# 32 columns of the second expert sweep move from dense to gathered, and the fifth row buffer moves into a tile of the middle stage

## The chip, the cores and the metric

The kernel runs on one core of one Trainium2 chip. Its engines are TensorE (PE; the loading of its weights is shown apart, as PEld), VectorE (DVE), ScalarE (ACT), GpSimd (POOL), and SyncE (SP), which here only issues transfers; 16 DMA engines move data between HBM and SBUF. The metric is the time of one execution on the device in microseconds (us), as a median of runs.

## The reference, cut to what matters

One encoder layer over 256 tokens of 2048 columns: an attention block, and then a mixture of 16384 one-neuron experts, of which every token uses 128 (8 heads, 16 each). The change lies in the last step, the sum of the experts' value rows:

```
u = jnp.take(expert_u, eb, axis=0)
vv = jnp.take(expert_v, eb, axis=0)
act = jax.nn.gelu(jnp.einsum('td,thkd->thk', xb, u))
return jnp.einsum('thk,thkd->td', act * gb, vv)
```

`expert_v` has 16384 rows of 2048 float32 columns. The layer ends with a residual add and an RMS norm.

## The kernel before

The stages are: input projection and attention; output projection; query projection and the search for each token's 128 experts; the first sweep, over `expert_u`; the middle stage, which turns the sums of the first sweep into one gated weight for each token and expert; and the second sweep, over `expert_v`.

**The second sweep has two halves.** The first `V1` = 1472 columns of `expert_v` are done densely: the kernel keeps a weight matrix over all 16384 experts in the arena `A` (zero where a token does not use an expert), and TensorE multiplies every expert's row by it. The other `VT` = 576 columns are done sparsely: for each of the 2 token tiles and each of a token's 128 picks, an indirect DMA gathers 128 rows (one for each token of the tile) and VectorE adds them, weighted, to a running sum.

**Dense half.** The 1472 columns are three chunks, of widths `VW` = (512, 512, 448). There are 192 units of loading (`units` = 128 blocks of experts x 3 chunks / 2). Three successive units hold two expert blocks: a unit of 1024 columns, one of 2 x 448 = 896 (`i % 3 == 1`), and another of 1024. `load_split` brings a unit into one of five `raw` buffers (SP issues it), ACT rounds it to `hi`, DVE makes `lo = raw - hi`; there are three buffers of each. Then `v_matmuls` issues 12 matmuls for a unit: two token tiles, two halves of the unit, and three products (lines 939 to 941: weight high part by `hi`, the same by `lo`, weight low part by `hi`). Over the sweep the 448-wide chunk takes 128 blocks x 2 tiles x 3 products = 768 matmuls. The six sums stay in PSUM until the end.

**Sparse half.** `fetch` takes a row buffer from the pool tile `rows` (`ROWS` = 5 buffers of 128 x 576) and issues the gather on POOL (line 649). `weigh` (line 1020) is one DVE instruction: it multiplies a landed row buffer by a column of `wN` and adds it to `vsum`. Right behind it `weigh` calls `fetch` again, so that five gathers are in flight at most, and each waits for the weighing that frees its buffer. The first five are fetched at unit `FETCH` = 4, each behind a one-column memset (`held`).

**Order.** DVE's order is written out by hand in this stage (`tc.manual_schedule(engines={DVE})`): after each unit's `lo`, `spread` puts in as many `weigh` steps as an even spread of the 256 over the remaining units gives, one or two each. DVE runs them in that order, so a `weigh` that waits for its row holds up the `lo` behind it. The other engines' orders come from the scheduler.

**The tile of the middle stage.** `h2t` is a tile of 128 x 2 x 512 float32. The first sweep reads it; then the middle stage uses its space for four arrays of 256 columns: `partT` (columns 0 to 255), `actT` (256 to 511), `wT` (512 to 767) and `wN` (768 to 1023). The first three hold sums and weights of the middle stage and are not read in the second sweep. `wN` is read by every `weigh`. `weights_of(1)` reads columns 640 to 767 just before the second sweep's gathers begin.

**The end.** At unit `units - 5` the gathered sum goes to the output tile; the last three units' matmuls are ordered by token tile; then follow, for each tile and chunk, the residual add (line 1071), squares, gain, scaling (lines 238 and 240) and the store.

Of the kernel before, what the change touches and what calls it, by code (L numbers as in the profile page):

```python
# [9 lines left out]
F32 = mybir.dt.float32  # L10
# [8 lines left out]
P = 128  # L19
# [14 lines left out]
D1 = 1536  # L34
DT = D - D1
KA = D1 // P
V1 = 1472
VT = D - V1
VW = (512, 512, V1 - 1024)
RAW = 3  # L40
# [25 lines left out]
FETCH, WEIGH, ROWS = 4, 7, 5  # L66
# [37 lines left out]
def encoder_layer_kernel(ctx: ExitStack, tc: tile.TileContext, x, gT, w_in, gq, gk, w_out, g2,  # L104
# [27 lines left out]
    def take(n, at=None):  # L132
        if at is None:
            at = pos[0]
            pos[0] += n
        assert at + n <= NK * S, at + n
        return arena[:, at:at + n]
# [77 lines left out]
    def load_gain(g):  # L215
        nc.sync.dma_start(gb, bass.AP(tensor=g.tensor, offset=g.offset, ap=[[0, P], [1, D]]))

    def v_chunk(c):
        return slice(c * 512, c * 512 + VW[c]) if c < 3 else slice(V1, D)

    squares = Ring([arena[:, 20480 + VT * i:20480 + VT * (i + 1)] for i in range(2)])

    def square_sum(t, c, ss, at=chunk):
        src = xs[:, t, at(c)]
        nc.scalar.activation(squares.next()[:, :src.shape[-1]], src, AF.Square, accum_out=ss[:, c:c + 1])
# [65 lines left out]
    rows = Ring([take(512) for _ in range(3)])  # L291
# [210 lines left out]
    h2t = consts.tile([P, NT, DT], F32, name="h2t")  # L502
# [141 lines left out]
    def held(rows_):  # L644

        nc.vector.memset(rows_[:, 0:1], 0.0)

    def gather(rows_, table, t, j):
        nc.gpsimd.indirect_dma_start(out=rows_, out_offset=None, in_=table,  # L649
                                     in_offset=bass.IndirectOffsetOnAxis(ap=experts[:, j // 32, t * 32 + j % 32:t * 32 + j % 32 + 1], axis=0))  # L650
        return rows_
# [110 lines left out]
    rows, hots, hot, one_hots = {}, {}, {}, {}  # L762
# [19 lines left out]
    with query:  # L782
        for i in range(units):
# [20 lines left out]
            while ended and (ended[0][0] <= i or i == units - 1):  # L804
                _, dst, sums = ended.popleft()
# [12 lines left out]
            while opening and opening[0][0] <= i:  # L818
                p = opening.popleft()[1]
# [185 lines left out]
    vp = ctx.enter_context(tc.tile_pool(name="vp", bufs=2))  # L1005
    raws.append((vp, MORE))
    vsum = vp.tile([P, NT, VT], F32, name="vsum", bufs=1)
    picks, coming = deque((t, j) for t in range(NT) for j in range(P)), deque()

    def fetch(hold=False):  # L1010
        if picks:
            t, j = picks.popleft()
            rows_ = vp.tile([P, VT], F32, name="rows", bufs=ROWS)
            if hold:
                held(rows_)
            coming.append((t, j, gather(rows_, v_tail, t, j)))

    def weigh():
        t, j, rows_ = coming.popleft()
        nc.vector.scalar_tensor_tensor(vsum[:, t], rows_, wN[:, t, j:j + 1], vsum[:, t], op0=OP.mult, op1=OP.add)  # L1020
        fetch()
# [6 lines left out]
    with tc.manual_schedule(engines={DVE}):  # L1028
        for i in range(units):
# [15 lines left out]
            if i == 3 * units // 4:  # L1045
                nc.sync.dma_start(xs[:, :, :V1], x2d.rearrange("p (t d) -> p t d", t=NT)[:, :, :V1])
                load_gain(gf)
                ready_sqrt()
            if i == FETCH:
                for _ in range(ROWS):  # L1050
                    fetch(hold=True)
                nc.sync.dma_start(vsum, x2d.rearrange("p (t d) -> p t d", t=NT)[:, :, V1:])
            if WEIGH <= i < units - 1:
                spread(units - 7 - i)
            if i == units - 5:
                for t in range(NT):
                    nc.vector.tensor_copy(xs[:, t, V1:], vsum[:, t])
                    square_sum(t, 3, ssl[t], v_chunk)
# [98 lines left out]
```

## Time and profile before

| | |
|---|---|
| median of 3 runs | 1644.61 us (1644.09 to 1644.99) |
| the profiled execution | 1645.29 us |
| its span, first to last instruction | 1643.5 us |
| PE busy in the span | 1621.1 us |
| DVE busy in the span | 1357.2 us |
| POOL busy in the span | 702.7 us |
| matmuls of the second sweep | from 1123.4 to 1632.9 us |
| gathers of `expert_v` | from 1137.3 to 1602.3 us |

The span is read as follows. A profile's times are those of one execution, counted from its first instruction. An engine's busy time is the time in which it works on at least one instruction; successive matmuls overlap in the records, so the pace of TensorE is read from the starts of successive matmuls rather than from the duration of one. The share of the DMA engines is the mean share of the time in which the 16 have a packet under way.

### The profile page before, as it was taken

How to read it: one execution, taken by the hardware profiler on the slowest of the kernel's cores; microseconds unless marked ns; L12 is line 12 of the kernel's file. 1: busy time of each engine (PE TensorE's matmuls, PEld its weight loads, DVE VectorE, ACT ScalarE, POOL GpSimd, SP SyncE). 2: the span in 40 equal slices, each digit the busy share in tenths (PEclk: the TensorE clock that was granted, in tenths of full speed). 3: DMA queues.
4: the chain of work that ended last, by engine and by line, in shares of the span. 5: the costliest groups of instructions: out<-in, count | busy, mean ns of one | idle time of the engine just before them, and what ended most of it. 6: DMA issues, size and time to landing. Idle time of an engine off the chain costs nothing.

```text
span 1643.5 us, 25515 instructions
## 1 busy us (share of the span) xinstructions
PE 1621.1 (99%) x8706; PEld 1403.7 (85%) x8706; DVE 1357.2 (83%) x3043; ACT 866.7 (53%) x1255; POOL 702.7 (43%) x582
## 2 busy tenths in 40 slices
PE   8999999999999999999999999999999999999997
PEld 6888888887888888888888889998888888888886
DVE  6765555559799989888888859997999999999996
ACT  6465555454444454444444448996444444444444
POOL 0000000000233368776765623334677766666670
PEclk9999999999999999999999999999999999999999
DMA  7644554565776689999999873336999999999994
GB/s 250 194 142 165 166 205 154 192 219 174 240 252 244 238 295 376 372 343 346 338 341 317 296 249 116 120 127 206 375 384 361 365 345 361 355 356 346 356 349 153
DMA packets 126163, 443.04 MB, mean 270 GB/s; under 512 B 17745, under 2 KB 18641, under 8 KB 125649
## 3 DMA queue, kind: packets, MB, share of 16 engines
q1 hardware_dynamic: 85072, 298.78, 52.0%
q0 software_dynamic: 40960, 142.64, 24.4%
q8 instruction: 68, 1.11, 0.3%
q14 instruction: 63, 0.51, 0.1%
HBM read 437.02 MB, written 4.33 MB: 269 GB/s over the span
## 4 chain that ended last, share of the span: by engine, by line
PE 92%; DVE 4%; DMA 2%; ACT 1%; issue 1%; SPq 0%; ACTq 0%; DVEq 0%
PE act L797 21%; PE act L799 11%; PE o L940 10%; PE o L941 10%; PE o L939 10%; PE pr L275 6%; PE pr L277 6%; PE pr L276 6%; PE X L854 3%; PE W L904 3%; DVE lo L171 1%; PE o1p L860 1%; PE sc L357 1%; PE po L388 1%; DMA raw<-in_w_in_dram 1%
## 5 line engine op out<-in xcount | busy, mean ns | idle before, releaser
L170 ACT ACTIVATE hi<-raw 128x1024 fp32r<-128x1024 f32 (+1 forms) x445 | 464.8, 1045 | 528.7 <-PE o L941 252.4
L171 DVE TENSOR_TENSOR lo<-raw,hi 128x1024 fp32r<-128x1024 f32 (+1 forms) x445 | 535.5, 1204 | 176.0 <-ACT hi L170 173.7
L797 PE MATMUL act<-hTa,hi 128*128 128x512 f32 x1536 | 396.9, 393 | 0.0
L649 POOL DMA_INDIRECT rows<-in_v_tail_dram,experts x256 | 323.9, 1265 | 152.5 <-DVE vsum L1020 75.8
L649 POOL DMA_INDIRECT A<-in_u_tail_dram,experts x121 | 146.9, 1214 | 467.5 <-DVE den L637 409.0
L797 PEld LDWEIGHTS act<-hTa,hi 128*128 128x128 f32 x1536 | 271.5, 189 | 44.6
L940 PE MATMUL o<-lo,wt 128*128 128x512 f32 (+1 forms) x768 | 293.2, 382 | 0.8 <-DVE lo L171 0.7
L939 PE MATMUL o<-hi,wt 128*128 128x512 f32 (+1 forms) x768 | 293.2, 382 | 0.0
L941 PE MATMUL o<-hi,wt 128*128 128x512 f32 (+1 forms) x768 | 293.0, 382 | 0.0
L649 POOL DMA_INDIRECT wm<-in_u_tail_dram,experts x135 | 174.6, 1293 | 168.2 <-DVE wm L655 122.6
L799 PEld LDWEIGHTS act<-hTa,lo 128*128 128x128 f32 x1536 | 218.2, 190 | 21.0 <-DVE lo L171 0.2
L799 PE MATMUL act<-hTa,lo 128*128 128x256 f32 x1536 | 224.4, 282 | 0.0
L1020 DVE SCALAR_TENSOR_TENSOR vsum<-rows,h2t,vsum 128x576 f32<-128x576 f32 x256 | 208.8, 816 | 13.8 <-DMA rows<-in_v_tail_dram,experts 11.0
L940 PEld LDWEIGHTS o<-lo,wt 128*128 128x128 f32 x768 | 144.2, 188 | 25.6 <-DVE lo L171 1.3
L941 PEld LDWEIGHTS o<-hi,wt 128*128 128x128 f32 x768 | 144.2, 188 | 24.4 <-DVE wt L934 0.5
L939 PEld LDWEIGHTS o<-hi,wt 128*128 128x128 f32 x768 | 144.2, 188 | 24.1
L275 PE MATMUL pr<-hi,hTa 128*128 128x512 f32 x408 | 164.2, 404 | 0.0
L276 PE MATMUL pr<-lo,hTa 128*128 128x512 f32 x408 | 160.1, 392 | 0.3
L277 PE MATMUL pr<-hi,hTa 128*128 128x512 f32 x408 | 159.5, 391 | 0.0
L170 ACT ACTIVATE hi<-A 128x1024 fp32r<-128x1024 f32 x72 | 76.6, 1065 | 72.6 <-PE act L797 52.0
L171 DVE TENSOR_TENSOR lo<-A,hi 128x1024 fp32r<-128x1024 f32 x72 | 88.1, 1223 | 20.7 <-ACT hi L170 20.5
L897 POOL TENSOR_SCALAR o<-cs,I2T,h2t 128x128 f32<-128x128 f32 x64 | 54.7, 860 | 115.0 <-DVE h2t L888 56.6
(161 smaller groups left out, 2002.9 us busy)
## 6 DMA issues: line engine op xcount, KB each, us to landing
raw<-in_v_head_dram SPq DMA_DIRECT2D x128, 512.0 KB, 5.5
raw<-in_u_head_dram SPq DMA_DIRECT2D x120, 512.0 KB, 5.3
raw<-in_w_in_dram SPq DMA_DIRECT2D x72, 512.0 KB, 3.3
A<-in_u_head_dram SPq DMA_DIRECT2D x72, 512.0 KB, 5.3
raw<-in_v_head_dram SPq DMA_DIRECT2D x64, 448.0 KB, 5.8
raw<-in_w_out_dram SPq DMA_DIRECT2D x32, 512.0 KB, 3.3
raw<-in_w_query_dram SPq DMA_DIRECT2D x32, 512.0 KB, 3.7
bc<-i1d SPq DMA_DIRECT2D x32, 512.0 KB, 3.7
```

The source lines that it names most:

```text
L170: nc.scalar.activation(hi, raw, AF.Copy)
L171: nc.vector.tensor_tensor(lo, raw, hi.bitcast(F32), op=OP.subtract)
L275: nc.tensor.matmul(ps[t], xT(k, 0, r), hi[:, c], start=first, stop=False)
L276: nc.tensor.matmul(ps[t], xT(k, 0, r), lo[:, c], start=False, stop=False)
L277: nc.tensor.matmul(ps[t], xT(k, 1, r), hi[:, c], start=False, stop=last)
L649: nc.gpsimd.indirect_dma_start(out=rows_, out_offset=None, in_=table, in_offset=bass.IndirectOffsetOnAxis(ap=experts[:, j // 32, t * 32 + ...
L797: nc.tensor.matmul(ps, hi[:, c], h, start=k == 0, stop=False)
L799: nc.tensor.matmul(ps[:, :S], lo[:, c], hTs(k, 0, slice(0, S)), start=False, stop=k == KA - 1)
L939: nc.tensor.matmul(ps, w[:, 0, r], hi[:, c], start=e == 0, stop=False)
L940: nc.tensor.matmul(ps, w[:, 0, r], lo[:, c], start=False, stop=False)
L941: nc.tensor.matmul(ps, w[:, 1, r], hi[:, c], start=False, stop=e == NK - 1)
L1020: nc.vector.scalar_tensor_tensor(vsum[:, t], rows_, wN[:, t, j:j + 1], vsum[:, t], op0=OP.mult, op1=OP.add)
```

## The change

Three numbers follow from `V1`: the dense part has 1440 columns, its third chunk is 416 wide, and `VT`, the gathered part, is 608 wide. The unit `i % 3 == 1` is loaded as 832 columns, the rows of the gathered table are 2432 bytes long in place of 2304, and the boundary between the two parts of the output moves with them. The number of units, matmuls, gathers and weighings stays as it is. Four row buffers stay in the pool `vp`; the fifth is the first 608 columns of `h2t`, so it covers `partT`, `actT` and the first 96 columns of `wT`. A ring hands out the five in turn.

```
-V1 = 1472
+V1 = 1440
...
     vsum = vp.tile([P, NT, VT], F32, name="vsum", bufs=1)
+
+    row_bufs = Ring([vp.tile([P, VT], F32, name="rows", bufs=ROWS - 1) for _ in range(ROWS - 1)]
+                    + [h2t.rearrange("p t d -> p (t d)")[:, :VT]])
...
-            rows_ = vp.tile([P, VT], F32, name="rows", bufs=ROWS)
+            rows_ = row_bufs.next()
```

## Rows read from the trace of the kernel before

**Rows 1.** The page, its first part: busy time of each engine, share of the span, instructions.

```profile
PE 1621.1 (99%) x8706; PEld 1403.7 (85%) x8706; DVE 1357.2 (83%) x3043; ACT 866.7 (53%) x1255; POOL 702.7 (43%) x582
```

**Rows 2.** The page, its fourth part: the chain of work that ended last, share of the span by engine.

```profile
PE 92%; DVE 4%; DMA 2%; ACT 1%; issue 1%; SPq 0%; ACTq 0%; DVEq 0%
```

**Rows 3.** Four stretches of the second sweep: busy time of each engine and its instructions, then the granted TensorE clock, the share of the DMA engines and what they moved.

```profile
1160.00:1250.00 90.00, 90.00 (x412) 77.09 (x412) 81.83 (x95) 42.17 (x47) 63.33 (x50) 1.00 1.01 381
1250.00:1350.00 100.00, 100.00 (x458) 85.70 (x457) 92.07 (x107) 45.91 (x51) 70.72 (x56) 1.00 0.98 356
1350.00:1450.00 100.00, 100.00 (x458) 85.81 (x457) 92.92 (x107) 46.58 (x52) 69.48 (x56) 1.00 0.98 356
1450.00:1550.00 100.00, 100.00 (x458) 85.62 (x457) 91.94 (x106) 47.55 (x54) 67.21 (x56) 1.00 0.97 351
```

**Rows 4.** Groups of instructions by line and shape, 1120 to 1640 us: count, busy us, mean ns of one, idle time of the engine before them and what ended it.

```profile
L649 POOL DMA_INDIRECT rows<-in_v_tail_dram,experts x256 | 323.9, 1265 | 152.5 <-DVE vsum L1020 75.8 <-issue 43.4 <-DMA rows<-in_v_tail_dram,experts 11.7
L1020 DVE SCALAR_TENSOR_TENSOR vsum<-rows,h2t,vsum 128x576 f32<-128x576 f32 x256 | 208.8, 816 | 13.8 <-DMA rows<-in_v_tail_dram,experts 11.0
L940 PE MATMUL o<-lo,wt 128*128 128x512 f32 x512 | 199.7, 390 | 0.8 <-DVE lo L171 0.7
L171 DVE TENSOR_TENSOR lo<-raw,hi 128x1024 fp32r<-128x1024 f32 x126 | 154.0, 1223 | 34.2 <-ACT hi L170 33.3
...
L940 PE MATMUL o<-lo,wt 128*128 128x448 f32 x256 | 93.5, 365 | 0.0
...
L171 DVE TENSOR_TENSOR lo<-raw,hi 128x896 fp32r<-128x896 f32 x63 | 68.3, 1084 | 1.0 <-ACT hi L170 1.0
...
L238 ACT ACTIVATE A<-A,rstd 128x576 f32<-128x576 f32 x2 | 1.5, 768 | 0.0
...
L1071 DVE TENSOR_TENSOR A<-A,o 128x448 f32<-128x448 f32 x2 | 1.2, 614 | 0.0
```

**Rows 5.** Timeline of all engines from 1400 us (start us, us, what): the first of 24 matmuls of 512 columns, the first of the 12 of 448 columns behind them, and the next of 512.

```profile
1401.57 0.39 PE L939 MATMUL o<-hi,wt 128*128 128x512 f32 x1
...
1407.02 0.36 PE L939 MATMUL o<-hi,wt 128*128 128x448 f32 x1
...
1409.45 0.39 PE L939 MATMUL o<-hi,wt 128*128 128x512 f32 x1
```

**Rows 6.** Timeline of TensorE in the first sweep, from 900 us: eight matmuls of 256 columns in one row, and the row behind it.

```profile
901.76 1.11 PE L799 MATMUL act<-hTa,lo 128*128 128x256 f32 x8
902.71 1.09 PE L797 MATMUL act<-hTa,hi 128*128 128x512 f32 x4
```

**Rows 7.** Groups of weight loads over the whole span: the loads of those 256-column matmuls.

```profile
L799 PEld LDWEIGHTS act<-hTa,lo 128*128 128x128 f32 x1536 | 218.2, 190 | 21.0 <-DVE lo L171 0.2
```

**Rows 8.** What DVE waited for, 1160 to 1250 us: us in total, times, longest.

```profile
DVE vsum L1020 <- DMA rows<-in_v_tail_dram,experts: 5.6, 6, 1.9
```

**Rows 9.** The same, 1300 to 1500 us.

```profile
DVE vsum L1020 <- DMA rows<-in_v_tail_dram,experts: 1.5, 3, 0.5
```

**Rows 10.** Timeline of DVE around 1224 us: a weighing that waited for its row, and the `lo` of a 448-wide unit behind it.

```profile
1223.53 0.82 DVE L1020 SCALAR_TENSOR_TENSOR vsum<-rows,h2t,vsum 128x576 f32<-128x576 f32 x1 [1.94 <-DMA rows<-in_v_tail_dram,experts]
1224.26 1.08 DVE L171 TENSOR_TENSOR lo<-raw,hi 128x896 fp32r<-128x896 f32 x1
```

**Rows 11.** Timeline of TensorE there: the first matmul that reads that `lo`.

```profile
1225.83 0.37 PE L940 MATMUL o<-lo,wt 128*128 128x448 f32 x1
```

**Rows 12.** Transfers, 1160 to 1250 us: the sum, and the gathers with the median time from issue to landing.

```profile
DMA packets 9267, 34.31 MB, mean 381 GB/s; under 512 B 1364, under 2 KB 1364, under 8 KB 9132
...
rows<-in_v_tail_dram,experts POOLq DMA_INDIRECT x50, 6.8
```

**Rows 13.** The same, 1300 to 1500 us.

```profile
DMA packets 19780, 70.89 MB, mean 354 GB/s; under 512 B 2981, under 2 KB 2981, under 8 KB 19766
...
rows<-in_v_tail_dram,experts POOLq DMA_INDIRECT x111, 6.0
```

**Rows 14.** Transfers, 1150 to 1600 us: the sum, and each queue's packets, MB and share of the 16 engines' time (q1: the dense units; q0: the gathers).

```profile
DMA packets 44842, 161.72 MB, mean 359 GB/s; under 512 B 6714, under 2 KB 6714, under 8 KB 44681
...
q1 hardware_dynamic: 25152, 88.85, 52.3%
q0 software_dynamic: 19657, 72.47, 45.9%
```

**Rows 15.** All waits of 1120 to 1643 us: the longest of a matmul of the second sweep for its `lo`.

```profile
PE o L940 <- DVE lo L171: 0.7, 1, 0.7
```

**Rows 16.** What writes and reads the arena `A`, 700 to 980 us: duration min/median/max, first and last start; and, after the list of what these instructions waited for, the gathers' time to landing.

```profile
L649 POOL DMA_INDIRECT A<-in_u_tail_dram,experts x76: 945/1152/1937, 700.4 to 918.6; - x76
...
L803 ACT ACTIVATE A<-act x66: 380/400/411, 702.9 to 976.7; 128x256 f32<-128x256 f32 x66
...
  PE act L799: 42.2, 33
...
DMA to landing us min/median/max: 3.9/5.8/7.8
```

**Rows 17.** The two transposes of `wT` by `weights_of` (whole span).

```profile
L909 PE MATMUL wtp<-cs,h2t x2: 272/274/275, 1059.8 to 1130.8; 128*128 128x128 f32 x2
```

**Rows 18.** What writes and reads the row buffers (whole span).

```profile
L649 POOL DMA_INDIRECT rows<-in_v_tail_dram,experts x256: 942/1402/1942, 1137.3 to 1602.3; - x128
L1020 DVE SCALAR_TENSOR_TENSOR vsum<-rows,h2t,vsum x256: 805/812/882, 1144.0 to 1609.8; 128x576 f32<-128x576 f32 x128
```

## The prediction

> **What bounds the kernel now.** I read the page first: TensorE is busy 99% of the span and carries 92% of the chain that ended last [rows 1, 2]. Such a share is an average over stages, so the next view is the second sweep by stretches: PE fills every one of them, 100 us of 100, at the granted clock of 1.00, full speed (2.4 GHz) [rows 3]. Then the waits: from 1120 us to the end a matmul waited once for its `lo`, 0.7 us [rows 15]. So the sweep runs at TensorE's own pace, and a shorter matmul shortens it, as long as nothing else becomes late. Two things are near it. DVE is busy 92.07, 92.92 and 91.94 us of 100, and the DMA engines show a share of 0.97 to 1.01 [rows 3]. The rest of the reading is about these two.
>
> **The matmuls: minus 10.2 us.** The duration of one matmul overlaps the next, so I take starts. 24 matmuls of 512 columns take 1407.02 - 1401.57 = 5.45 us, 227 ns each; the 12 of 448 take 1409.45 - 1407.02 = 2.43 us, 202.5 ns each [rows 5]. That is 24.6 ns for 64 columns, 12.3 for 32. The 256-column matmuls of the first sweep start 0.95 / 8 = 118.8 ns apart [rows 6], so from 256 to 448 columns the slope is 83.7 / 192, or 13.95 ns for 32 columns. The new width, 416, lies between 256 and 448, near the upper end; 32 columns at 2.4 GHz would be 13.3 ns, which lies between both slopes, and I take it. 768 matmuls x 13.3 = 10.2 us; ends 9.4 and 10.7. One thing could put a floor under it: a weight load takes 190 ns, about as long as the 189 ns that a 416-column matmul would have. But the 256-column matmuls have loads of 190 ns too [rows 7] and still start 119 ns apart, so loads overlap each other and there is no such floor. PE waits nowhere in the sweep, so all of it lies on the path.
>
> **DVE: plus 4.4 us of work, off the path.** `lo` takes 1223 ns for 1024 columns and 1084 for 896 [rows 4]: 1.09 ns a column. The 256 weighings grow by 32 columns, 256 x 35 = 8.9 us; the 64 `lo` of the narrow unit shrink by 64 columns, 64 x 70 = 4.5 us. Net 4.4 us, about 0.9 for each 100 us of today. In the settled stretches DVE is idle 7.7 us of 100; afterwards the same work has 98.0 us (a group of three units takes 7.88 us today and 7.72 then) and 93.2 of busy time, so 4.8 stay idle. On average it fits. ACT gets less work in the sweep and is half idle.
>
> **Gathers on POOL: nothing.** The number is the same and the issue takes 1265 ns whatever its rows' length, as far as rows show; with 256 weighings between 1144.0 and 1609.8, one each 1.83 us [rows 4, 18], 1.79 afterwards, POOL keeps up. It has nothing else to do there.
>
> **Transfers: more, on engines that look full.** Dense units lose 64 x 128 x 64 columns x 4 B = 2.1 MB, gathers gain 256 x 128 x 32 x 4 B = 4.2 MB: plus 2.1 MB in a stretch that is to be 2% shorter. 354 GB/s in the settled sweep [rows 13] become about 367. A share near 1.00 doesn't tell the ceiling: from 1160 to 1250 us, where the `raw` buffers are still being filled up, the same mix moved 381 GB/s [rows 12], against 354 with a share of 0.98 later. So 367 is under what this sweep has shown over 90 us, by 14 GB/s in place of 27.
>
> The Trainium skill, "DMA: Bandwidth & Descriptors", section "Specifications", gives an HBM limit of about 358 GB/s for a core; the 381 GB/s of this trace speaks against it as a ceiling here. By it the transfers would be the bound already, and the change would lengthen them (the first rival). The same page, "How a descriptor splits into AXI transactions", says that a read that doesn't start on a multiple of 256 bytes fetches from the boundary below. Rows of 2304 bytes all start on one; of rows of 2432 bytes every other one doesn't. By its table's counting that makes 78 beats a row where the bytes alone make 76; no row of this trace has such a start, so nothing here shows it.
>
> **What the fuller engines cost: plus 1.0 us.** Where the engines moved 381 GB/s, rows landed 6.8 us after issue in place of 6.0 [rows 12, 13], and DVE waited for rows 5.6 us in 90, against 1.5 in 200 [rows 8, 9]. Such a wait holds up the `lo` queued behind it, and PE waits for that. The cover is the lead of the three `hi`/`lo` buffers. At 1223.53 a weighing waited 1.94 us; the `lo` behind it ended at 1225.34, 0.5 us before its matmul [rows 10, 11]. So a single wait is hidden, barely, and what counts is whether DVE has the time for the sum. In that 90 us stretch DVE is busy 81.8 and idle 8.2 [rows 3]. Afterwards it is 88.2 us long with 82.7 of work: 5.5 idle. The row waits there, 5.6 x 2432/2304 = 5.9, would be 0.4 us too many. And the stretch lasts longer: filling the buffers took (381 - 354) x 90 us = 2.4 MB of surplus, and at 14 GB/s that takes some 170 us. 0.4 x 170/88 is 0.8; over the whole sweep it would be 2.0. I take 1.0. The ends are 0 (leads absorb it) and 14.8, for row waits half as long again (8.4 us) from the first unit to the last: 2.9 too many in each 88 us, over 450 us.
>
> **The fifth buffer: nothing.** Its columns were last read before the gathers: the transposes of `wT` are done at 1131.1, the first gather starts at 1137.3 [rows 17, 18]. The number of buffers stays five, the turn is the same. The end: the last chunk's add shrinks from 614 ns by some 35, the scaling of the gathered part (768 ns) grows by as much [rows 4]; a tenth of a us either way.
>
> **The sum.** The profiled execution took 1645.29 us, 1643.5 of them span; the median is 0.7 lower. 1643.5 - 10.2 + 1.0 = 1634.3 of span, and with the same 1.1 us from span to median 1635.4.
>
> **Rivals.** First, the transfers pace the sweep (0.11). They moved 161.7 MB from 1150 to 1600 us at shares that add to 98.5% with the instruction queues [rows 14]. If that is full, the ceiling is 364.5 GB/s, 163.8 MB take 449.4 us, and nothing is gained: 1644.0, no change. For it speaks the share; against it the 381 of 1160 to 1250 us. By the 358 GB/s of the Trainium skill's page named above it would be 457.5 us, some 1652; by its two further beats a row, at 364.5 GB/s, some 1650.
>
> Second, on the other side, the row waits set the pace through DVE (0.10): the upper end above, 1644.6 - 10.2 + 14.8 = 1649.2, slower by 0.3%. It is decided by the landing of rows. Five buffers turn over once in 5 x 1.79 = 8.95 us; a weighing takes 0.81 and POOL starts 0.30 later; so a median landing above 7.8 us makes every weighing wait. Today's 6.0 to 6.8 speak against it; that the margin shrinks from both sides speaks for it.
>
> Third, the fifth buffer doesn't do what it says (0.02): were `h2t` guarded as a whole, each weighing's read of `wN` would wait for the last gather into it, some 51 times about 6 us, or 300 us: 1935. Against it: gathers of 5.8 us land in parts of `A` while ACT writes other parts, and what these wait for is a matmul [rows 16].
>
> Fourth, a matmul of 416 columns starts no closer than one of 448 (0.03): 1644.6 + 1.0, no change; rows 6 speak against it.
>
> **How the numbers follow.** The forecast has 0.74. With the stall anywhere from 0 to about 7 us it reaches from 1633.9 to 1641, all of it faster by over 0.2%, which is 3.3 us and about what a measurement of this kernel can tell from no change. Faster 0.74; the same 0.11 + 0.03 = 0.14; slower 0.10 + 0.02 = 0.12. The range goes down to 1633.5 (10.7 us gained, no stall, a little off the end) and up to 1644.5, which takes in the first rival and leaves out the second, the third and the fourth, 0.15.
>
> **What would show it.** Right: starts of 416-column matmuls 188 to 190 ns apart, a group of three units every 7.72 us, PE still 100 of 100 in each stretch, DVE some 95 of 100, 365 GB/s or more, row landings under 7.5 us, and row waits of 15 to 30 us in all. Wrong: idle time of PE ended by `lo` adding up to more than 3 us, or a rate that stays at 355 GB/s while ACT waits for `raw`. If PE waits while rows land late, the second rival; if ACT waits for `raw`, the first; if each fifth weighing waits, the third.

## The result and the profile after

The changed kernel takes 1634.96 us (median of 5 runs, 1633.52 to 1636.21), against 1644.95 us for the kernel before (1644.09 to 1646.85): a ratio of 0.9938, with a 95% interval of 0.9928 to 0.9949. That is 10.0 us gained; 9.2 were forecast. The profiled execution took 1634.96 us with a span of 1633.2.

The page of after, first and fourth part (busy time by engine; chain that ended last):

```profile
PE 1610.9 (99%) x8706; PEld 1401.9 (86%) x8706; DVE 1357.0 (83%) x3043; ACT 863.3 (53%) x1255; POOL 722.1 (44%) x582
...
PE 85%; DMA 6%; DVE 4%; issue 2%; POOL 1%; ACT 1%; SPq 0%; ACTq 0%; DVEq 0%; POOLq 0%
```

PE lost 10.2 us of busy time with the same 8706 matmuls [rows 1]. The chain says something that the busy times don't: TensorE's share of it fell from 92% [rows 2] to 85%, and DMA stands for 6%. Between 1130 and 1630 us the chain now runs through landing rows for 15.2% of the time, 13.7 in the pool's buffers and 1.5 in the fifth; before, it ran through none. The row gathers have become a second path beside TensorE's.

The pace of TensorE, in its timeline (the first 416-column matmul of a group of three units, the first of 512 columns behind its twelve, and the first of 416 in the next group):

```profile
1401.37 0.35 PE L939 MATMUL o<-hi,wt 128*128 128x416 f32 x1
...
1403.61 0.40 PE L939 MATMUL o<-hi,wt 128*128 128x512 f32 x1
...
1409.07 0.35 PE L939 MATMUL o<-hi,wt 128*128 128x416 f32 x1
```

Twelve matmuls take 2.24 us, 186.7 ns each, where those of 448 columns took 202.5 [rows 5]; a group takes 7.70 us in place of 7.88.

The second sweep by stretches (busy time of PE, PEld, DVE, ACT, POOL; granted clock, DMA share, GB/s):

```profile
1160.00:1250.00 90.00, 89.77 (x420) 78.26 (x420) 82.50 (x95) 41.45 (x46) 66.15 (x50) 1.00 1.01 387
1250.00:1350.00 100.00, 99.66 (x464) 86.39 (x463) 93.40 (x107) 45.97 (x52) 76.05 (x56) 1.00 0.99 361
1350.00:1450.00 100.00, 100.00 (x468) 87.05 (x468) 94.67 (x109) 46.46 (x52) 74.36 (x57) 1.00 0.99 368
1450.00:1550.00 100.00, 100.00 (x466) 86.76 (x465) 93.96 (x109) 48.06 (x54) 77.44 (x57) 1.00 0.99 365
```

Against [rows 3], DVE is 1.3 to 2 points fuller, the engines move 361 to 368 GB/s in place of 351 to 356, and for the first time PE doesn't fill its stretches quite. What DVE and PE waited for, from 1120 us to the end (us, times, longest):

```profile
DVE vsum L1023 <- DMA rows<-in_v_tail_dram,experts: 19.7, 36, 1.6
...
DVE vsum L1023 <- DMA h2t<-in_v_tail_dram,experts: 4.9, 8, 1.2
...
PE o L940 <- DVE lo L171: 1.2, 3, 0.8
```

Row waits are 24.6 us, where they were 11.0 [rows 4]; the second row is the fifth buffer's, 8 of 44 waits, about its share. Transfers from 1300 to 1500 us:

```profile
DMA packets 20070, 72.90 MB, mean 365 GB/s; under 512 B 3015, under 2 KB 3015, under 8 KB 20055
...
rows<-in_v_tail_dram,experts POOLq DMA_INDIRECT x90, 6.7
```

354 GB/s have become 365, and rows land after 6.7 us in place of 6.0 [rows 13].

Here is one wait to its end, in the timelines of DVE and of TensorE:

```profile
1221.09 0.85 DVE L1023 SCALAR_TENSOR_TENSOR vsum<-rows,h2t,vsum 128x608 f32<-128x608 f32 x1 [1.63 <-DMA rows<-in_v_tail_dram,experts]
1221.85 1.02 DVE L171 TENSOR_TENSOR lo<-raw,hi 128x832 fp32r<-128x832 f32 x1
```

```profile
1222.35 0.35 PE L939 MATMUL o<-hi,wt 128*128 128x416 f32 x1
1222.93 0.46 PE L940 MATMUL o<-lo,wt 128*128 128x416 f32 x1 [0.23 <-DVE lo L171]
```

A wait of 1.63 us; the `lo` behind it ends at 1222.87; its matmul starts at 1222.93, 0.58 us behind the one before it where 0.19 is the pace. In [rows 10, 11] a longer wait, 1.94 us, left 0.5 us to spare. The record calls 0.23 us idle, but 0.39 were lost: a matmul's recorded duration runs past the start of the next. So stalls are read from starts.

The whole sweep, from the first to the last matmul's start:

```profile
L939 PE MATMUL o<-hi,wt x768: 344/389/496, 1121.7 to 1622.3; 128*128 128x512 f32 x128, 128*128 128x416 f32 x64
...
L941 PE MATMUL o<-hi,wt x768: 345/389/505, 1122.6 to 1622.7; 128*128 128x512 f32 x128, 128*128 128x416 f32 x64
```

It takes 501.0 us, where before it took 1632.9 - 1123.4 = 509.5: 8.5 gained. The shorter matmuls alone give 768 x 15.8 ns = 12.1. So about 3.5 us are given back inside the sweep, and 1.7 of the span's gain lie ahead of the sweep, which began that much earlier.

### The profile page after: what moved, and what is told of

It reads as the page before. It is cut to its first block, busy times and chain, and to the rows that moved or that the text cites. A ratio compares the mean times of both kernels' runs of the same rounds, so it can differ in the third digit from the quotient of the medians.

```text
span 1633.2 us, 25511 instructions
## 1 busy us (share of the span) xinstructions
PE 1610.9 (99%) x8706; PEld 1401.9 (86%) x8706; DVE 1357.0 (83%) x3043; ACT 863.3 (53%) x1255; POOL 722.1 (44%) x582
## 3 DMA queue, kind: packets, MB, share of 16 engines
q0 software_dynamic: 40960, 146.83, 24.6%
## 4 chain that ended last, share of the span: by engine, by line
PE 85%; DMA 6%; DVE 4%; issue 2%; POOL 1%; ACT 1%; SPq 0%; ACTq 0%; DVEq 0%; POOLq 0%
PE act L797 22%; PE act L799 11%; PE o L941 7%; PE o L940 7%; PE o L939 7%; PE pr L277 7%; PE pr L276 7%; PE pr L275 7%; DMA rows<-in_v_tail_dram,experts 4%; PE X L854 3%; PE W L904 3%; DVE lo L171 1%; PE o1p L860 1%; POOL rows L649 1%; PE sc L357 1%
## 5 line engine op out<-in xcount | busy, mean ns | idle before, releaser
L649 POOL DMA_INDIRECT rows<-in_v_tail_dram,experts x205 | 276.4, 1348 | 100.9 <-DVE vsum L1023 50.3
L940 PE MATMUL o<-lo,wt 128*128 128x512 f32 (+1 forms) x768 | 289.3, 377 | 1.3 <-DVE lo L171 1.2
L939 PE MATMUL o<-hi,wt 128*128 128x512 f32 (+1 forms) x768 | 289.4, 377 | 0.5 <-ACT hi L170 0.5
L941 PE MATMUL o<-hi,wt 128*128 128x512 f32 (+1 forms) x768 | 289.7, 377 | 0.1
L1023 DVE SCALAR_TENSOR_TENSOR vsum<-rows,h2t,vsum 128x608 f32<-128x608 f32 x205 | 175.0, 854 | 21.1 <-DMA rows<-in_v_tail_dram,experts 19.7
```

The lines of the kernel that those rows point to most:

```text
L939: nc.tensor.matmul(ps, w[:, 0, r], hi[:, c], start=e == 0, stop=False)
L940: nc.tensor.matmul(ps, w[:, 0, r], lo[:, c], start=False, stop=False)
L941: nc.tensor.matmul(ps, w[:, 1, r], hi[:, c], start=False, stop=e == NK - 1)
```

## The experiments

Twelve kernels ran, four at a time on one chip, each beside the kernel before. The chips of the second and third four ran every kernel some 4 to 5 us longer (the kernel before: 1650.14 and 1648.88 us), and their sweeps began at 1126.6 to 1130.4 us; so ratios are compared, and lengths within the sweep. In the table, "over" is the sweep's length less 509.5 - 64 x (7.887 - group), what it would be at TensorE's own pace (7.887 us is the mean of 55 groups in the chain of before, 1149.59 to 1583.35 us). It is good to 1 or 2 us, since the wait for the first dense units differs by that much between executions. "Stalls" leaves this wait out: it is worked out from the starts of all 2304 matmuls, and adds up, behind 1160 us, by how much an interval exceeds the usual one of its width, where it does so by over a quarter. "Row waits" are those from 1120 us to the end.

| run | dense, gathered, buffers | ratio to before, 95% interval | sweep us | group us | over us | stalls us | row waits us |
|---|---|---|---|---|---|---|---|
| before | 1472, 576, 5 | 1 | 509.5 | 7.89 | 0 | 0.1 | 11.0 |
| after | 1440, 608, 5 | 0.9938, 0.9928 to 0.9949 | 501.0 | 7.70 | 3.5 | 2.3 | 24.6 |
| a0 | the same | 0.9939, 0.9928 to 0.9951 | 499.3 | 7.70 | 1.8 | 1.6 | 21.4 |
| a1 | the same | 0.9952, 0.9939 to 0.9966 | 500.5 | 7.70 | 3.0 | 2.5 | 23.8 |
| e1 | 1472, 576, 5 (one in `h2t`) | 1.0003, 0.9995 to 1.0012 | 509.1 | 7.89 | 0 | 0.1 | 12.3 |
| e2 | 1440, 576, 5 | 0.9930, 0.9917 to 0.9943 | 498.3 | 7.70 | 0.8 | 0.5 | 19.3 |
| e3 | 1472, 608, 5 | 0.9996, 0.9988 to 1.0005 | 509.5 | 7.89 | 0 | 0.2 | 17.6 |
| e4 | as e1, rows 128 bytes later | 0.9997, 0.9983 to 1.0010 | 509.4 | 7.89 | 0 | 0.1 | 11.5 |
| e5, e5b | 1440, 608, 6 | 0.9920, 0.9899 to 0.9942; 0.9928, 0.9915 to 0.9941 | 500.7; 498.7 | 7.70 | 3.2; 1.2 | 0.2; 0.4 | 0.3; 0.2 |
| e6 | 1408, 640, 5 | 0.9944, 0.9924 to 0.9965 | 504.3 | 7.59 | 13.8 | 10.3 | 21.8 |
| e7 | 1440, 608, 4 | 1.0210, 1.0176 to 1.0244 | 547.9 | 7.70 | 50 | 40 | 63.9 |
| e8 | 1408, 640, 6 | 0.9906, 0.9891 to 0.9921 | 492.2 | 7.59 | 1.7 | 1.6 | 1.2 |
| e9 | 1376, 672, 6 | 0.9891, 0.9874 to 0.9907 | 487.8 | 7.44 | 7.1 | 6.0 | 1.7 |

A stall can cost twice. In e7 TensorE waited 3.5 us for a `lo`, and behind this wait the granted clock was 0.50, the lower of its two levels (1.2 GHz): a stretch of e7 (columns as in the stretches above) and the matmul that had waited.

```profile
1192.00:1196.00 4.00, 4.00 (x10) 3.13 (x10) 3.96 (x5) 0.00 (x0) 2.83 (x2) 0.50 1.01 384
...
1191.08 0.79 PE L940 MATMUL o<-lo,wt 128*128 128x512 f32 x1 [3.53 <-DVE lo L171]
```

Matmuls of 512 columns start 427 ns apart there, 227 at 1.00. Four such stretches in e7 cost some 7.7 us, one each in e5 and e6, behind waits at the sweep's head, some 1.6; the other sweeps have none. This is in "over" and not in "stalls".

**a0 and a1: the changed kernel again.** No edit.

> The changed kernel as it is, beside the others on one chip. Reading of its first profile: a group of three units takes 7.70 us in place of 7.887 (64 x 0.187 = 12.0 us gained), stalls of TensorE in the sweep give back about 3, and the sweep began 1.7 us earlier for reasons that lie in the first microseconds of the execution. If that early start is a variation between executions, the median stays within 1 us of 1635 and the ratio to the kernel before within 0.993 to 0.995, and in another profile the sweep's first matmul may start 1 to 2 us later.

1635.66 us on the first chip. The sweep began at 1124.9 us in this execution, 3.2 us later than in the first profile of the same kernel, so the early start there is a variation between executions, not an effect of the change.

> The changed kernel as it is, on the chip of the next three, to compare them with. Theory: ratio to the kernel before 0.993 to 0.995, TensorE's group 7.70 us, 1.5 to 3 us of stalls behind the sweep's first groups, each with a row wait ahead of it.

1641.03 us beside 1648.88. The ratio of 0.9952 lies a little outside the expected range; its interval reaches into it.

**e1: the fifth buffer's place alone.**

```
-V1 = 1440
+V1 = 1472
```

> The fifth buffer in the middle stage's tile alone; the widths are those of before (1472 dense, 576 gathered). Theory (the buffer's place costs and gives nothing): ratio 1.000 within 0.001, 1644 to 1646 us, a group every 7.887 us, row waits on DVE near the 11 us of before. Rival (the place matters, because the weighing reads its weights from the same tile): every fifth weighing waits for its neighbour's gather, row waits of tens of us or more, and the time rises by over 5 us.

No difference: 1645.18 us beside 1645.28, row waits 12.3 us. The place costs nothing and gives nothing but room: the weighing reads its weights from the same tile without waiting for gathers into the rest of it.

**e2: the dense part alone.**

```
 VT = D - V1
+VG = 576
...
-    ... vp.tile([P, VT], F32, name="rows", ...
+    ... vp.tile([P, VG], F32, name="rows", ...
...
-        nc.vector.scalar_tensor_tensor(vsum[:, t], rows_, ... , vsum[:, t], ...
+        nc.vector.scalar_tensor_tensor(vsum[:, t, :VG], rows_, ... , vsum[:, t, :VG], ...
```

> The dense part alone: 1440 dense columns, while the gathered rows stay 576 wide, so the expert sums of the last 32 columns are left out. Theory (TensorE's pace is the gain, and the wider gathers give back about 3 us through row waits): 12 us less than before, 1633 us, ratio 0.9925 to 0.9935, a group every 7.70 us, DVE waits for rows of at most 15 us, stalls of TensorE under 1.5 us. Rival (what is given back comes from the shorter sweep itself, with buffers turning over faster, not from the width): stalls stay at about 3 us and the time at 1635.

1633.76 us beside 1645.28: 11.5 gained, and 0.8 us over. So the shorter sweep by itself brings the gain almost without the stalls. One number missed: row waits are 19.3 us, not at most 15. The faster turn alone thus makes most of the added waits. That they are nearly harmless here because DVE has less to do is not shown: the gathers also move 4.2 MB less than in a0 (364 GB/s against 372 from 1160 to 1590 us), and no run changes only one of the two.

**e3: the wider gathers alone.** Rows of 608 columns from column 1440, and a dense part of 1472.

```
-V1 = 1440
+V1 = 1472
 VT = D - V1
+VG = 608
...
-        nc.vector.tensor_copy(xs[:, t, V1:], vsum[:, t])
+        nc.vector.tensor_copy(xs[:, t, V1:], vsum[:, t, VG - VT:])
```

> The gathers alone: rows of 608 columns are gathered and weighed, while the dense part keeps 1472 columns; 32 columns are worked on by both, and the gathered sums of those 32 are dropped. Theory (DVE's 9 us more work and 4.2 MB more transfers lie beside TensorE's work as long as its group takes 7.887 us): ratio 1.000 to 1.001, 1645 to 1646 us, stalls of TensorE under 1 us, though row waits double to 20 us. Rival (wider gathers cost time by themselves, by the transfers' rate): 2 to 4 us more than before, with TensorE waiting for lo.

1645.07 us beside 1645.28. The 9 us more of DVE's work and the 4.2 MB cost nothing while a group takes 7.89 us, though the engines moved 368 GB/s from 1160 to 1590 us, nearly the changed kernel's 370. The two halves alone make -11.5 and -0.2 us, and together, on the same chip, -9.6. By the medians alone that is not clear of the noise (the intervals of e2 and a0 overlap); the stalls, 0.5 and 0.2 us alone and 1.6 together, say the same: what is given back belongs to the two together.

**e4: rows that start 128 bytes later.**

```
-    in_=table,
+    in_=table, element_offset=32,
...
-        "v_tail": a["peer_v"][0][:, V1:],
+        "v_tail": _np.pad(a["peer_v"][0][:, V1:].ravel(), (32, VT - 32)).reshape(-1, VT),
```

> Widths of before (1472 dense, 576 gathered, 2304 bytes a row), fifth buffer in the middle stage's tile, and the gathered table begins 128 bytes later, so that no row starts on a multiple of 256 bytes, where in the kernel before all do. (In the changed kernel every other row does.) Theory (the start of a row doesn't matter): the share of the gathers' queue from 1160 to 1600 us, the rows' time to landing (6.0 to 6.2 us) and the time (1645) stay as they are. Rival: the share of that queue and the landing rise by some 5%, row waits on DVE grow from 11 us towards 20, and the time stays within 2 us, since TensorE's pace hides it. The Trainium skill, DMA: Bandwidth & Descriptors, section How a descriptor splits into AXI transactions, would have the rival: by its counting 76 beats a row in place of 72.

Nothing moved. Transfers of e4, 1150 to 1600 us:

```profile
DMA packets 44926, 162.08 MB, mean 360 GB/s; under 512 B 6730, under 2 KB 6730, under 8 KB 44765
q1 hardware_dynamic: 25143, 88.87, 52.3%
q0 software_dynamic: 19750, 72.81, 45.9%
```

Both shares are those of [rows 14]. By the Trainium skill ("DMA: Bandwidth & Descriptors", section "How a descriptor splits into AXI transactions") a row has 76 beats in place of 72, and by an estimate from that, if time goes by beats, the gathers' share should have risen by some 5%; this trace doesn't show it. (Where the table itself begins is not in the trace; and the rows' time to landing isn't in this profile.)

**e5 and e5b: a sixth buffer.** The tiles `I1T`, `I2T` and `GT` of the middle stage become one tile, whose first 608 columns are the sixth buffer.

```
-FETCH, WEIGH, ROWS = 4, 7, 5
+FETCH, WEIGH, ROWS = 4, 7, 6
...
-    I1T = consts.tile([P, S], F32, name="I1T")
...
+    picked = consts.tile([P, 3, S], F32, name="picked")
+    I1T, I2T, GT = (picked[:, i] for i in range(3))
...
-                    + [h2t.rearrange("p t d -> p (t d)")[:, :VT]])
+                    + [b.rearrange("p t d -> p (t d)")[:, :VT] for b in (h2t, picked)])
```

> The changed kernel with a sixth row buffer, made of the three tiles of the middle stage that hold the picks' indices and gates (now one tile). Theory (row waits on DVE, from landings of 6.7 us against a turn of five buffers in 8.95, cause the stalls): the turn becomes 10.7 us, row waits fall from 25 us to under 8, stalls of TensorE from about 3 us to under 1, 1632 to 1633 us. Rival (the transfers' rate causes the stalls): row waits fall, but ACT waits longer for raw, and the time stays at 1635.

> The changed kernel with six row buffers again. Its first run had row waits of 0.3 us in place of 22 to 25, and no stall behind the sweep's first group, but its times were taken where every kernel was some 5 us longer and scattered more. Theory: 1.5 to 3 us less than the changed kernel on the same chip, ratio to the kernel before 0.991 to 0.993. Rival (the sixth buffer's earlier gathers delay the first dense units, and that takes back what the stalls gave): the same as the changed kernel within 1 us, with the first groups of the sweep over 2 us longer.

Row waits are gone. The first run's profile still has 3.2 us over, but most of it at the sweep's head (its timeline of TensorE; there is no later wait of PE in the sweep):

```profile
1145.75 0.51 PE L938 MATMUL o<-hi,wt 128*128 128x512 f32 x1 [1.19 <-issue]
1147.01 0.50 PE L939 MATMUL o<-lo,wt 128*128 128x512 f32 x1 [0.76 <-issue]
```

These wait for the first dense units; the kernel before has such a gap of 0.7 us there [rows 15], and the size varies. The sixth buffer isn't what makes them longer: e6, with five, has 1.4 and 0.8. The other part is a granted clock of 0.50 right behind them (in all of 1149 to 1151 us), which costs some 1.6 us. In the second run 1.2 us are over, and its one row wait is this:

```profile
DVE vsum L1022 <- DMA rows<-in_v_tail_dram,experts: 0.2, 1, 0.2
```

On the same chip it takes 1636.91 us and the changed kernel 1641.03, 4.1 less where 1.5 to 3 were expected; the ratios' intervals (0.9915 to 0.9941 and 0.9939 to 0.9966) barely overlap. The stalls behind 1160 us, 2.5 us in a1 and 0.4 here, account for half of it; the rest is within what these intervals leave open. The two, from 1160 to 1590 us (columns as above):

```profile
1160.00:1590.00 430.00, 429.03 (x2001) 373.65 (x2000) 403.45 (x462) 200.80 (x224) 328.78 (x240) 1.00 1.00 369
1160.00:1590.00 430.00, 430.00 (x2011) 376.19 (x2010) 408.54 (x465) 201.05 (x225) 309.74 (x242) 1.00 1.00 372
```

So five buffers' row waits are what stalls the changed kernel, and not the transfers' rate, which is 369 GB/s in a1 and 372 in e5b.

**e6: one step further with five buffers.**

```
-V1 = 1440
+V1 = 1408
```

> One step further: 1408 dense columns, 640 gathered, five buffers as in the changed kernel. Theory (the row ring sets the pace once TensorE's group falls below what it can follow): TensorE alone would give another 10 to 12 us, but stalls grow to 6 to 12 us, each ended by lo, and row waits to over 35 us; 1630 to 1637 us. Rival (stalls stay at some 3 us): 1623 to 1625. Rival (the transfers are full): over 1640, with a rate under 372 GB/s and ACT waiting for raw.

Ratio 0.9944; the 1643.28 us themselves lie above the expected range, on a chip where the kernel before takes 1650.14. TensorE's group falls to 7.59 us and would gain 7 us more; 13.8 us are over (some 1.6 of them the lower clock), and at the median all of the step is lost, though this kernel scatters: its 8 times reach from 1636.16 to 1644.61 us. It is the first theory, with two misses: more is lost than the 6 to 12 us of stalls that it had, and row waits are 21.8 us, not over 35. The engines moved 372 GB/s from 1160 to 1590 us and ACT waited 10.6 us for dense units (1150 to 1600 us), so this run alone doesn't refute full transfers; e8, at the same width, does. A reading that no run tests: where TensorE stalls, the weighings are spread over a longer time, so a row has longer to land.

**e7: four buffers.**

```
-FETCH, WEIGH, ROWS = 4, 7, 5
+FETCH, WEIGH, ROWS = 4, 7, 4
...
-    row_bufs = Ring([... bufs=ROWS - 1) for _ in range(ROWS - 1)] + [h2t. ...
+    row_bufs = Ring([... bufs=ROWS) for _ in range(ROWS)])
```

> The changed kernel with four row buffers, without the one in the middle stage's tile. Theory (five buffers are just enough): four turn over in 7.2 us, less than landing, weighing and issue take together (6.7 + 0.85 + 0.3 = 7.85), so nearly every weighing waits, row waits grow past 60 us and TensorE stalls by 15 to 45 us; 1648 to 1680. Rival (rows land faster when fewer are under way, and the wait is hidden): landing under 5.5 us, less than 5 us lost, 1635 to 1640.

1686.01 us beside 1650.14, slower by 2.1%. What DVE and PE waited for, 1150 to 1600 us:

```profile
DVE vsum L1022 <- DMA rows<-in_v_tail_dram,experts: 56.6, 75, 2.8
PEld o L940 <- DVE lo L171: 32.1, 34, 4.0
PE o L940 <- DVE lo L171: 19.2, 21, 3.5
```

Here the whole path is in the records: a row, the weighing, the `lo`, the matmul. Of the 50 us over, some 7.7 are the lower clock behind long waits; the other 43 or so lie within the 15 to 45 us of the theory, and the row waits of the whole sweep are 63.9 us. A miss: 84 of the 256 weighings waited, not nearly all. The engines moved 336 GB/s from 1160 to 1590 us; they weren't the limit. This is the second rival of the prediction in full size, one buffer away.

**e8 and e9: six buffers and fewer dense columns.** The edit of e5 with `V1` = 1408 and 1376.

> 1408 dense columns, 640 gathered, six row buffers. With five buffers this width lost some 11 us to stalls behind the sweep's first groups. Theory (those were the row ring's): a group takes 7.59 us, stalls are under 3 us, and the time is 8 to 10 us under the changed kernel's: ratio to the kernel before 0.986 to 0.990. Rival (the transfers' rate sets a ceiling near 372 GB/s, which the five-buffer run at this width also moved): the stalls stay, now with ACT waiting for raw, ratio 0.992 to 0.996, and rows wait little.

> 1376 dense columns, 672 gathered, six row buffers. TensorE's group would be some 7.43 us, the demand on transfers near 390 GB/s, DVE's work some 7.3 us in each group. Theory: DVE and the transfers are both at their end, stalls of 10 us and more, ratio 0.988 to 0.994, and this width is no better than 1408. Rival (TensorE still sets the pace): another 8 us, ratio 0.982 to 0.984.

Both beat the changed kernel: 1632.92 and 1631.49 us on the chip where it takes 1641.03 and the kernel before 1648.88. For e8 the theory holds (1.7 us over, row waits 1.2, 8.1 us under the changed kernel; the ratio of 0.9906 lies a little outside the expected range, its interval reaches into it), and the rival's ceiling doesn't: it moved 382 GB/s from 1160 to 1590 us. In e9 the same view gives 389, and TensorE begins to stall, for another reason. The two stretches, e8 and e9, and then waits of e9, 1150 to 1600 us:

```profile
1160.00:1590.00 430.00, 429.47 (x2034) 372.93 (x2033) 417.16 (x472) 200.85 (x229) 321.06 (x244) 1.00 1.01 382
1160.00:1590.00 430.00, 428.51 (x2054) 366.10 (x2053) 421.93 (x474) 199.62 (x231) 331.77 (x247) 1.00 1.02 389
```

```profile
ACT hi L170 <- PE o L940: 176.4, 130, 2.5
...
ACT hi L170 <- DMA raw<-in_v_head_dram: 35.1, 21, 4.5
ACT hi L170 <- DVE lo L171: 16.7, 13, 2.0
```

ACT waits 35.1 us for dense units, where it waited 3.9 in the changed kernel, 14.0 in e5b and 15.9 in e8: now dense units are late. That the transfers' rate makes them late is not shown. DVE is busy 421.9 us of 430, and a dense unit is loaded only when a `lo` has freed its buffer: from 1250 to 1580 us SP waited 252.7 us in all for that. So a full DVE would make late units as well, and no run separates the two. With 7.1 us over, fewer than the 10 of the theory, the step from 1408 to 1376 gains 1.4 us at the median, and the two intervals overlap; which of the two is better stays open.

## Why the prediction was right, point by point

**What bounds the kernel** was read rightly: TensorE's pace in the second sweep. e2 shows it alone: 32 columns fewer in 768 matmuls, 11.5 us.

**The matmuls**: forecast 10.2 us, measured 12.1. The mechanism holds and there is no floor from weight loads, but the term was mis-sized: 416 columns start 186.7 ns apart, not 189. Neither end of the range held it (13.95 ns for 32 columns; it was 15.8). The later widths show where the step lies: 384 columns start 175.8 ns apart (twelve from 1302.74 to 1304.85 in e8), 352 some 162.5 (1321.88 to 1323.83 in e9). Successive steps of 32 columns are 15.8, 10.9 and 13.3 ns, with 12.3 from 512 to 448. On an even line from 512 to 352 columns, 448 stands 1.3 ns above and 416 1.6 below, so the one step between them is larger than either slope that the range came from. Why they stand there the runs don't show.

**DVE**: forecast some 95 busy of 100, measured 93.4 to 94.7. That its fuller time is what makes row waits matter fits e2 and e3, which don't prove it.

**Gathers on POOL**: forecast nothing, with an issue of 1265 ns whatever the rows' length. In the changed kernel an issue takes 1346 ns on average, in e5 with the same rows and six buffers 1282. POOL keeps up, and what the longer issue adds to the turn of the ring no run separates.

**Transfers**: forecast 367 GB/s, measured 361 to 368, with landings of 6.7 us (under 7.5). The first rival, transfers as the bound at 364.5 GB/s, is refuted: the changed kernel moved 369 to 372 GB/s over 430 us, and e9 389. The limit of about 358 GB/s for a core in the Trainium skill ("DMA: Bandwidth & Descriptors", section "Specifications", half of what it gives for a stack that two cores share) doesn't hold as a ceiling for this kernel, which runs on one core: the measurement decides.

**What fuller engines cost**: forecast 1.0 us with ends 0 and 14.8, measured 1.8 to 3.5 over in three profiles of the kernel, 1.6 to 2.5 of it stalls behind the sweep's head. The step was right (row waits, 21 to 25 us as forecast, hold up the `lo` behind them), the size too small. The sum took DVE's idle time over 88 us against the waits over 88 us, as if waits and idle time could be exchanged freely. They can't: the order on DVE is fixed, and one wait of 1.6 us stalls TensorE if the lead is short just then. Nor did the waits end with the fill of the `raw` buffers: from 1300 to 1500 us DVE still waited 11.1 us for rows (1.5 before, [rows 9]). Most of the stalls did lie where the forecast put them: 1.3 to 1.7 us between 1160 and 1330 us, where it had 0.8.

Two errors of opposite sign, 1.9 us too little gained and 0.8 to 2.5 too little given back, left the total within 1 us. The forecast's sum was better than its terms.

**The fifth buffer**: nothing, as forecast (e1). The third rival is refuted, and so is the fourth.

**The second rival**, row waits as the pace, wasn't decided by the median landing, as the text had it (7.8 us), but sooner and by degrees: at 6.7 it costs some 2 to 3 us, with 640 columns some 12, and with four buffers some 43, the lower clock left out.

**The mark for "wrong"** was ill-chosen: idle time of PE ended by `lo` is 1.2 us in the record where starts give 2.3.

## What to carry to other kernels

Moving work from the bounding engine to a ring of transfers paid one for one here only while the ring turned over well above what landing, weighing and issue take together. With five buffers the turn of 8.95 us against some 7.85 at the median already cost 2 to 3 us, with six, 10.7 us, next to nothing. So measure the three against buffers times the interval, before the step and after it, and count the later step's interval. Here one more buffer was worth more than the next 32 columns: with five the step to 1408 columns was lost, with six it was gained. And when the trace's chain begins to name a second engine, as the gathers here with 6%, the next step of the same kind may no longer be the same step.

## What the runs showed of the hardware that was not expected

- The interval of matmuls doesn't fall evenly with their columns: 227, 202.5, 186.7, 175.8 and 162.5 ns for 512, 448, 416, 384 and 352 columns, each with a weight load of some 188 ns beside it. From 416 columns down the load takes longer than the interval, and the intervals go on falling.
- Dense units and gathered rows, mixed, moved 354 GB/s at a DMA share of 0.98 (before), 372 at 1.00 (e5b) and 389 at 1.02 (e9). A share near 1 said nothing about how much more would go through.
- Rows gathered from starts 128 bytes later cost the same share of the DMA engines, 45.9%.
- A stall of TensorE by a late row can cost more than its length: in e7 the granted clock fell from 1.00 to 0.50 at or behind four waits of 1.5 to 3.5 us, and at 0.50 matmuls of 512 columns start 427 ns apart in place of 227. Other waits in the same run had no such stretch behind them; what decides it these runs don't show.
